# Silu of r at the PSUM banks, key-value products of a head pair in one run, and a token-major end of a hybrid decoder step

## The chip, the cores and the metric

The kernel runs on one core of a Trainium2 chip. The metric is the device time of one execution in microseconds. A profiled execution also has a span, from its first to its last instruction on the core, which is a little shorter than its device time. The engines are called as in the profile: PE does the matrix products (PEld its weight loads), DVE the vector operations, ACT the activation functions, POOL further vector operations without access to PSUM, and SP issues the DMAs.

## What is computed

One inference step of one decoder layer, for 2048 prompt tokens and 8 x 4 sample tokens, width 1024, all in fp32. The mixer projects the normed input into q, k, v, r, a, u and sv. Four heads of gated linear attention run over q, k, v with a decay made from a; four heads of spatial gating run over u and sv.

```
q, k, v, r, a, u, sv = split_cols(xn @ w_in)
logg = log_sigmoid(a @ w_alpha + b_alpha) / GLA_TAU
S_t = diag(exp(logg_t)) S_{t-1} + k_t^T v_t;   o_t = q_t S_t
o = rmsnorm(o, g_gla_out) * silu(r)
z = causal position mixing of rmsnorm(gelu(sv)) within 128 positions;   s_out = gelu(u) * z
h = x + concat(o, s_out) @ w_out
h = h + attention of rmsnorm(h) over 256 memory tokens
c = causal convolution of width 3 of (rmsnorm(h) @ w_gate)
y = rmsnorm(h + (gelu(c) * (rmsnorm(h) @ w_up)) @ w_down, g_final)
```

Besides y, the outputs are the last states of the linear attention, the last two rows of the gate projection, the memory keys and values, and the normed sv of the sample tokens.

## The kernel before, in words

The prompt is worked off in four blocks of 512 tokens (`SB`, `s` = 0 to 3); the 32 sample tokens ride along with block 1 in the mixer and with block 2 in the feed-forward part. Activations lie feature-major, 128 features by 512 tokens to a tile, in eight tiles `B.h[0..7]`. Every large product is made of three products of split fp32 numbers (`mm3`, L92 to L94). A few projections are token-major: `tm_steps` holds four PSUM banks, one for each 128 tokens (c = 0 to 3), and adds up over eight k tiles in four steps (j = 0 to 3) before each bank is evacuated by `evac`. sv, v and r are such projections; r is evacuated by `scaled`, a DVE scaling with the token's rstd.

PSUM has two pools of four banks: `acc` (tag "acc") for the large projections and `mps` (tag "mm") for everything else. SBUF tiles come from pools too: `U` with 49 buffers, `T_` with 6. A new tile of a pool waits until a buffer of that pool is given back.

The linear attention of a block is the list of `gla_steps`. For each pair of heads, p = 0 and 1: `diag`, seven `level`s and `decay` make the local score matrix P (per head), the decayed queries qz (per head), the decayed and transposed keys kt and the chunk decays eb. Then `chunk(p, c)` runs four times, once per 128 tokens: the output products P v and qz S into one "mm" bank (`op`), a DVE copy into B.o, the key-value products kt v of the two heads into another "mm" bank (`kv`), each on 64 of the bank's partitions, and one DVE operation that makes the next state S. The tail (`gtail`) follows: `onorm` squares and sums o, `silu(c)` applies Silu to r in SBUF, `gate(c)` multiplies, `back(h)` transposes the four heads to feature-major `cat[0..3]`. The spatial gating gives `cat[4..7]` through `mix(h)` (`zp`, z, then the split `ch`, `cl`).

The order of the work is written out as a list of steps. `weave` puts the steps of side lists (the gates, the chunks, the mixing, the tail) between the steps of the main list proj + w1, at given places; `run` calls the steps in that order and issues weight loads ahead of them, up to AHEAD = 5 units of cost. The tile framework takes this order as priority and settles at build the order of each engine's instructions by its own estimate of times (`schedule_with_timeline_sim=True`); on the chip each engine and each DMA queue runs its list in that fixed order. The output projection's first half `w1` (`a_wo`, contraction over cat[4..7]) stands right behind the last r step and takes "acc" banks, its second half needs cat[0..3].

The small product for a (`a_fn`, `ap`) gives the decay's input. It is inserted before the last step of sv and takes an "acc" bank. At the start of the program `late_constants` scales the weights for it (wa) on DVE, eight small operations, from a tile loaded by DMA (war).

At the end of block 3 the feed-forward groups go gate, up, down; the last group of two feature tiles is `down_last`: for each half of 256 tokens eight products' groups (feature-major, 256 columns) are added to h, and `final_steps` transposes the half's tokens to PSUM (`yp`), squares them, makes the rstd, scales by it and by g_final and writes y. The last two gate rows (`carry`) are transposed (`ncp`), copied and written by `conv_out_steps`, six steps, ahead of that.

Of the kernel before, what the change touches and what calls it, by code (L numbers as in the profile page):

```python
# [19 lines left out]
D = 1024  # L20
# [17 lines left out]
def hymba_step_kernel(  # L38
# [22 lines left out]
    def U(name, dt=F32):  # L61
        return up.tile([128, TM], dt, tag="U", name=name)
# [7 lines left out]
    def acc(name):  # L70
        return accp.tile([128, 512], F32, tag="acc", name=name)
# [318 lines left out]
    def gcol(nm, k):  # L390
        return cols_of[nm][:, k:k + 1]
# [11 lines left out]
    def late_constants():  # L403
# [15 lines left out]
        for k in range(8):  # L419
            dve.tensor_scalar(wa[:, k, 0:16], war3[:, k], gcol("gmix", k), None, ALU.mult)  # L420

# [384 lines left out]
    def proj_steps(B):  # L806
# [28 lines left out]
        def a_fn():  # L835
            B.aT = T_(f"aT{s}")
            for ci, (c0, cw) in enumerate(chunks_of(sample)):
                ps = acc(f"ap{s}{ci}")
                for k in range(8):
                    pe.matmul(ps[hr[k % 4], :cw], wa[:, k], B.h[k][:, c0:c0 + cw], start=k < 4, stop=k >= 4)  # L840
                act.activation(B.aT[:, c0:c0 + cw], ps[:, :cw], AF.Copy)

        out = tm_steps(w, SV0, xs, sample, ev_tm("sv", lambda o, i, f: act.activation(o, i, AF.Gelu_apprx_tanh, scale=f)), f"ws{s}")
        out.insert(3, Step(a_fn))
        out.append(fm_step(w, K0, xs, sample, ev_fm("k", 0, times), f"wk{s}"))
# [74 lines left out]
    def gla_steps(B):  # L920
# [6 lines left out]
        def gates():  # L927
# [24 lines left out]
            B.lg = lg  # L952
            B.P, B.qz, B.kt, B.eb, B.kms, B.b = {}, {}, {}, {}, {}, {}

# [118 lines left out]

        def chunk(p, c):
            if p == 0 and c == 0:
                B.o = [U(f"o{s}{i}") for i in range(nt)]
            ps = mps(f"op{s}{p}{c}")
            S = state[p]
            cs = slice(c * 128, (c + 1) * 128)
            for hh in range(2):  # L1080
                h = 2 * p + hh
                os_ = slice(hh * 128, (hh + 1) * 128)
                pe.matmul(ps[:, os_], B.P[h][:, cs], B.v[c][:, h * 128:(h + 1) * 128], start=True, stop=False)
                pe.matmul(ps[:, os_], B.qz[h][:, cs], S, start=False, stop=True)
            dve.tensor_copy(B.o[c][:, p * 256:(p + 1) * 256], ps[:, :256])
            kv = mps(f"kv{s}{p}{c}")
            for hh in range(2):
                h = 2 * p + hh
                pe.matmul(kv[hh * 64:(hh + 1) * 64, :128],
                          B.kt[p][:, c * 128 + hh * 64:c * 128 + (hh + 1) * 64],  # L1090
                          B.v[c][:, h * 128:(h + 1) * 128], start=True, stop=True)
            Sn = cp.tile([128, 128], F32, tag=f"S{p}", name=f"S{s}{p}{c}", bufs=2)
            dve.scalar_tensor_tensor(Sn, S, B.eb[p][:, c:c + 1], kv[:, :128], ALU.mult, ALU.add)
            state[p] = Sn
            if s == NSB - 1 and c == 3:
                nc.sync.dma_start(o_state_gla[0, 0, 2 * p:2 * p + 2].rearrange("hh d v -> (hh d) v"), Sn)

# [41 lines left out]

        def silu(c):  # L1140
            n = 128 if c < 4 else NS
            act.activation(B.r[c][:n, :512], B.r[c][:n, :512], AF.Silu)

        def gate(c):
# [311 lines left out]

    def ffn_steps(B, fin=None):
        s, sample = B.s, B.ffn_sample
# [87 lines left out]

        def down_last(f0, half_of):

            def step(half, ws):
                cs = slice(half * 256, (half + 1) * 256)  # L1550
                for m in range(8):
                    wh, wl = ws[m // 4]
                    ms = slice((m % 4) * 128, (m % 4 + 1) * 128)
                    ps = acc(f"d{s}{f0}{m}{half}")
                    for k in range(2):
                        hi, lo = acts[f0 + k]
                        mm3(ps[:, :256], wh[:, k, ms], wl[:, k, ms], hi[:, cs], lo[:, cs], k == 0, k == 1)
                    dve.tensor_tensor(B.h[m][:, cs], ps[:, :256], B.h[m][:, cs], ALU.add)

            def fn(*ws):  # L1560
                for half in range(2):
                    step(half, ws)
                    for st in half_of(half):
                        st.fn()
            return Step(fn, [wready(wdd[f0, 4 * j], f"wd{s}{f0}{j}") for j in range(2)])

# [24 lines left out]
        for f0, nf in GROUPS:  # L1591
            for i in range(0, nf, 2):
                j = (f0 + i) // 2
                here = pend if i == 0 else []
                main += [g_(j), u_(j)] + here if nf == 2 else [g_(j)] + here + [u_(j)]
            if fin and nf == 2:
                pend = [down_last(f0, lambda half: fin[2 * half:2 * half + 2])]
            else:
                pend = [down(f0, nf, m) for m in range(0, 8, 8 // nf)]
# [58 lines left out]
    for s, B in enumerate(blocks):  # L1658
# [18 lines left out]
        steps += weave(sc + x1, (turns[:2], 4, 5), (turns[2:], 8, 8))  # L1677
        fin = final_steps(B)
        fstart, fmain, flast = ffn_steps(B, fin if s == NSB - 1 else None)
        steps += x2 + [xstat, fstart]  # L1680
        sides = []
        if B.mix_sample:
            sides.append((sample_steps(), 1, len(fmain) - 5))
        steps += weave(fmain[:-4], *sides)
        after = fin
        if s + 1 < NSB:
            nxt = blocks[s + 1]
# [39 lines left out]
```

## Time and profile before

| what | us |
|---|---|
| median of 3 runs (range) | 2845.88 (2843.69 to 2846.43) |
| the profiled execution | 2846.04 |
| its span | 2844.3 |
| PE busy | 2814.4 (99%) |
| PEld busy | 2457.6 (86%) |
| DVE busy | 1773.6 (62%) |
| ACT busy | 1047.0 (37%) |
| POOL busy | 542.4 (19%) |

A row of a timeline has the start, the duration, the engine, the line, the operation and its tiles (out<-in), the shape and a count when equal neighbours are merged; in brackets stands the engine's idle time just before it and who ended it. The duration of a product is from its start to its modelled end and overlaps the next one's; the pace of PE is read from the starts. L92 to L94 are the three products of `mm3`. PEclk is the granted clock of PE as a share of the full one.

### The profile page before, as it was taken

Reading aid. Unit: us, or ns where it says so; the run is one execution under the profiler, and the core shown is the slowest. Engines: PE = TensorE matmul, PEld = TensorE weight load, DVE = VectorE, ACT = ScalarE, POOL = GpSimd, SP = SyncE. Lnnn points to the kernel's source line nnn. Section 1 sums busy time; section 2 is a strip of 40 time slices with the busy share of each in tenths; the row PEclk is TensorE's granted clock in tenths of the full one; section 3 lists DMA queues with packets and bytes.
Section 4 is the critical chain, followed back from the end, with each engine's and each line's share of the span. In section 5 each row is a group of like instructions: output and inputs, shape, how many; then the busy total and the mean of one; then the engine's idle time right before and its main releaser. Section 6 shows DMA issues by size and latency. Waiting matters only on the chain.

```text
span 2844.3 us, 45766 instructions
## 1 busy us (share of the span) xinstructions
PE 2814.4 (99%) x17366; PEld 2457.6 (86%) x17366; DVE 1773.6 (62%) x3160; ACT 1047.0 (37%) x1942; POOL 542.4 (19%) x617
## 2 busy tenths in 40 slices
PE   8999999999999999999999999999999999999998
PEld 8788888888888898898888888899999888899998
DVE  6577468777657735555555773666666674565555
ACT  5536334333363424222124443422223543331221
POOL 1002113111110211322220021322221012131221
PEclk9999999999999999999999999999999999999999
DMA  9656679999932245888994215577776323577784
GB/s 304 207 156 199 208 228 332 335 340 329 345 112 77 94 153 178 302 284 291 329 344 161 73 60 181 191 259 257 257 263 213 104 69 119 185 258 269 273 286 173
DMA packets 363920, 625.54 MB, mean 220 GB/s; under 512 B 26730, under 2 KB 235724, under 8 KB 363702
## 3 DMA queue, kind: packets, MB, share of 16 engines
q1 hardware_dynamic: 363702, 622.62, 64.6%
q8 instruction: 138, 2.26, 0.3%
q14 instruction: 80, 0.66, 0.1%
HBM read 497.21 MB, written 125.31 MB: 219 GB/s over the span
## 4 chain that ended last, share of the span: by engine, by line
PE 95%; DVE 2%; DMA 1%; ACT 1%; issue 1%; POOL 0%; SPq 0%; DVEq 0%; POOLq 0%; ACTq 0%
PE d L92 6%; PE d L94 6%; PE d L93 6%; PE a_wo L92 2%; PE a_wo L94 2%; PE a_wo L93 2%; PE sc L94 2%; PE sc L93 2%; PE sc L92 2%; PE a_wx L93 2%; PE a_wx L94 2%; PE a_wx L92 2%; PE s L1022 2%; PE a_wg L92 1%; PE a_wup L92 1%; PE a_wg L93 1%
## 5 line engine op out<-in xcount | busy, mean ns | idle before, releaser
L92 PE MATMUL d<-acth,whi_wd 128*128 128x512 f32 (+2 forms) x720 | 244.6, 340 | 0.5 <-DVE h L1581 0.5
L93 PE MATMUL d<-actl,whi_wd 128*128 128x512 f32 (+2 forms) x720 | 242.5, 337 | 0.0
L94 PE MATMUL d<-acth,wlo_wd 128*128 128x512 f32 (+2 forms) x720 | 242.0, 337 | 0.0
L1581 DVE TENSOR_TENSOR h<-d,h 128x512 f32<-128x512 f32 (+1 forms) x232 | 133.4, 582 | 139.6 <-PE d L94 139.4
L1520 POOL TENSOR_TENSOR c<-c,bc_f 128x512 f32<-128x512 f32 (+1 forms) x88 | 138.5, 1578 | 137.9 <-ACT c L1519 137.2
L94 PEld LDWEIGHTS d<-acth,wlo_wd 128*128 128x128 f32 x720 | 135.4, 188 | 15.3 <-issue 1.2
L92 PEld LDWEIGHTS d<-acth,whi_wd 128*128 128x128 f32 x720 | 135.3, 188 | 14.4 <-DVE h L1581 0.7
L93 PEld LDWEIGHTS d<-actl,whi_wd 128*128 128x128 f32 x720 | 135.6, 188 | 13.8 <-issue 0.4
L1510 ACT ACTIVATE c<-g,colsb 128x512 f32<-128x512 f32 x88 | 71.7, 815 | 203.7 <-DVE g L1479 151.8
L1542 POOL TENSOR_TENSOR c<-r_q_wup,c 128x512 f32<-128x512 f32 (+1 forms) x33 | 59.1, 1790 | 333.5 <-DVE r_q_wup L279 213.1
L92 PE MATMUL a_wo<-ch,h_wo 128*128 128x512 f32 (+1 forms) x320 | 112.7, 356 | 4.5 <-DVE r L828 4.5
L1507 POOL COPY carry<-g 128x2 f32<-128x2 f32 x88 | 30.7, 349 | 436.5 <-DVE g L1479 434.4
L94 PE MATMUL a_wo<-ch,l_wo 128*128 128x512 f32 (+1 forms) x320 | 112.4, 353 | 0.0
L93 PE MATMUL a_wo<-cl,h_wo 128*128 128x512 f32 (+1 forms) x320 | 112.0, 351 | 0.0
L1511 DVE SCALAR_TENSOR_TENSOR c<-g,colsb,c 128x512 f32<-128x512 f32 x88 | 86.0, 977 | 29.3 <-ACT c L1510 28.8
L92 PE MATMUL sc<-whi_qk,woh 128*128 128x512 f32 x256 | 102.1, 399 | 0.0
L92 PE MATMUL a_wx<-pTh,whi_wx 128*128 128x512 f32 x256 | 101.3, 396 | 0.0
L94 PE MATMUL sc<-whi_qk,wol 128*128 128x512 f32 x256 | 101.1, 397 | 0.0
L93 PE MATMUL a_wx<-pTl,whi_wx 128*128 128x512 f32 x256 | 101.1, 395 | 0.0
L93 PE MATMUL sc<-wlo_qk,woh 128*128 128x512 f32 x256 | 101.0, 395 | 0.0
L94 PE MATMUL a_wx<-pTh,wlo_wx 128*128 128x512 f32 x256 | 100.6, 393 | 0.0
L84 ACT ACTIVATE acth<-c 128x512 fp32r<-128x512 f32 (+1 forms) x88 | 55.9, 636 | 110.4 <-DVE c L1542 85.0
(3369 smaller groups left out, 9204.8 us busy)
## 6 DMA issues: line engine op xcount, KB each, us to landing
whi_wd<-wd SPq DMA_DIRECT2D x66, 512.0 KB
wlo_wd<-wd SPq DMA_DIRECT2D x66, 512.0 KB
r_wo<-in_w_out_dram SPq DMA_DIRECT2D x32, 512.0 KB
whi_qk<-qkd SPq DMA_DIRECT2D x32, 512.0 KB
wlo_qk<-qkd SPq DMA_DIRECT2D x32, 512.0 KB
wlo_wx<-vod SPq DMA_DIRECT2D x32, 512.0 KB
whi_wx<-vod SPq DMA_DIRECT2D x32, 512.0 KB
r_wg<-in_w_gate_dram SPq DMA_DIRECT2D x22, 512.0 KB
```

Source lines behind the costliest of these rows:

```text
L84: act.activation(hi, src, AF.Copy)
L92: pe.matmul(ps, wh, xh, start=first, stop=False)
L93: pe.matmul(ps, wh, xl, start=False, stop=False)
L94: pe.matmul(ps, wl, xh, start=False, stop=last)
L1022: pe.matmul(ps3[:, :, c * 64:(c + 1) * 64], kl[:, c * 128:(c + 1) * 128], kr3[:, :, c * 64:(c + 1) * 64], start=True, stop=True)
L1507: pool.tensor_copy(carry[:, f, :], g[:, SB:SB + 2])
L1510: act.activation(c[:, :SB], g[:, 2:SB + 2], AF.Identity, bias=cb, scale=w2)
L1511: dve.scalar_tensor_tensor(c[:, :SB], g[:, 1:SB + 1], w1, c[:, :SB], ALU.mult, ALU.add)
L1520: pool.tensor_tensor(c[:, :T], c[:, :T], B.fbc[:, :T], ALU.mult)
L1542: (dve, pool)[i].tensor_tensor(c[:, :T], q[i], c[:, :T], ALU.mult)
L1581: dve.tensor_tensor(B.h[m + mm][:, cs], ps[:, :cw], B.h[m + mm][:, cs], ALU.add)
```

## The change

Six edits, all in the order or the place of work; the arithmetic is the same but for the end's order of sums.

1. r is evacuated by ACT with Silu, scaled by the token's rstd, straight from the "acc" bank. The DVE scaling and the `silu` steps of the tail are gone.
2. `chunk` becomes `states(p)` and `chunks(p, i)`. `states` does the key-value products of the four chunks of a pair, eight in a row, into one "mm" bank, then the four state updates; the states of the chunks live in a new tile of the U pool. `chunks` does the output products of two chunks into the two halves of one bank, and copies each half.
3. `a_fn` takes an "mm" bank and stands behind all of sv's steps.
4. wa is scaled by POOL instead of DVE.
5. The last down group of block 3 is made token-major: `turn_h` transposes h (before that group's part) to tokens through PSUM and ACT copies, between the steps of the group before; `last_rows` makes the down products with tokens on the partitions, 512 columns each, adds the turned h, sums the squares, and scales and writes a row tile while the next one is computed. For the last row tile, POOL multiplies the first half by g_final before the rstd is known, and ACT scales it.
6. Four of the six steps that write the last gate rows go between the gate and up steps of block 3, the other two behind the last full down group.

```diff
-            dve.tensor_scalar(wa[:, k, 0:16], war3[:, k], gcol("gmix", k), None, ALU.mult)
+            pool.tensor_scalar(wa[:, k, 0:16], war3[:, k], gcol("gmix", k), None, ALU.mult)
...
-                ps = acc(f"ap{s}{ci}")
+                ps = mps(f"ap{s}{ci}")
...
-        out.insert(3, Step(a_fn))
+        out.append(Step(a_fn))
...
-        out += tm_steps(w, R0, xs, sample, ev_tm("r", scaled), f"wr{s}")
+        out += tm_steps(w, R0, xs, sample, ev_tm("r", lambda o, i, f: act.activation(o, i, AF.Silu, scale=f)), f"wr{s}")
...
-        def chunk(p, c):
...
+        def states(p):
+            kv = mps(f"kv{s}{p}")
+            for c in range(4):
+                for hh in range(2):
+                    h = 2 * p + hh
+                    pe.matmul(kv[hh * 64:(hh + 1) * 64, c * 128:(c + 1) * 128],
+                              B.kt[p][:, c * 128 + hh * 64:c * 128 + (hh + 1) * 64],
+                              B.v[c][:, h * 128:(h + 1) * 128], start=True, stop=True)
+            t = U(f"S{s}{p}")
+            B.S[p] = [state[p]] + [t[:, c * 128:(c + 1) * 128] for c in range(3)]
+            state[p] = cp.tile([128, 128], F32, tag=f"S{p}", name=f"S{s}{p}e", bufs=2)
+            for c in range(4):
+                dve.scalar_tensor_tensor(B.S[p][c + 1] if c < 3 else state[p], B.S[p][c], B.eb[p][:, c:c + 1],
+                                         kv[:, c * 128:(c + 1) * 128], ALU.mult, ALU.add)
...
+        def chunks(p, i):
...
+            ps = mps(f"op{s}{p}{i}")
+            for j in range(2):
+                c = 2 * i + j
+                cs = slice(c * 128, (c + 1) * 128)
+                for hh in range(2):
+                    h = 2 * p + hh
+                    os_ = slice(j * 256 + hh * 128, j * 256 + (hh + 1) * 128)
+                    pe.matmul(ps[:, os_], B.P[h][:, cs], B.v[c][:, h * 128:(h + 1) * 128], start=True, stop=False)
+                    pe.matmul(ps[:, os_], B.qz[h][:, cs], B.S[p][c], start=False, stop=True)
+                dve.tensor_copy(B.o[c][:, p * 256:(p + 1) * 256], ps[:, j * 256:(j + 1) * 256])
...
-            out += [lambda p=p, c=c: chunk(p, c) for c in range(4)]
+            out += [lambda p=p: states(p)] + [lambda p=p, i=i: chunks(p, i) for i in range(2)]
...
-        tail = [onorm] + [lambda c=c: silu(c) for c in range(nt)] + [lambda c=c: gate(c) for c in range(nt)]
+        tail = [onorm] + [lambda c=c: gate(c) for c in range(nt)]
...
+        def turn_h(j):
+            for c in range(4):
+                ps = mps(f"hp{c}{j}")
+                for i in range(4):
+                    pe.transpose(ps[:, i * 128:(i + 1) * 128], B.h[4 * j + i][:, c * 128:(c + 1) * 128], ident)
+                t = U(f"ht{c}{j}")
+                act.activation(t[:, :512], ps, AF.Copy)
+                cur["ht", c, j] = t
...
+        def last_rows(*ws):
...
+            def finish(c, ss):
+                for j in range(2):
+                    y = cur["free"] if (c, j) == (2, 1) else T_(f"y{s}{c}{j}")
+                    if c == 3 and j == 0:
+                        act.activation(y[:, :512], early[:, :512], AF.Copy, scale=ss[:, 3:4])
+                    else:
+                        dve.scalar_tensor_tensor(y[:, :512], cur["ht", c, j][:, :512], ss[:, 3:4], gfin[j][:, :512],
+                                                 ALU.mult, ALU.mult)
+                    nc.sync.dma_start(y_prompt[0, s * SB + c * 128:s * SB + (c + 1) * 128, j * 512:(j + 1) * 512], y[:, :512])
...
+            for c in range(4):
...
+                    for k in range(2):
+                        hi, lo = acts[FT - 2 + k]
+                        mm3(ps, hi[:, cs], lo[:, cs], wh[:, k], wl[:, k], k == 0, k == 1)
...
+                    act.activation(junk, y[:, :512], AF.Square, accum_out=ss[:, j:j + 1])
+                    if c == 3 and j == 0:
+                        early = U("yg")
+                        pool.tensor_tensor(early[:, :512], y[:, :512], gfin[0][:, :512], ALU.mult)
...
+            ncs = conv_out_steps(carry, 2, o_state_conv[0, 0], "nc")
+            sides.append((ncs[:4], 30, 36))
...
-            steps += fmain[-4:] + conv_out_steps(carry, 2, o_state_conv[0, 0], "nc") + flast
+            steps += fmain[-4:-2] + flast[:1] + fmain[-2:] + ncs[4:] + flast[1:]
```

More of the change, by code (lines that the diff above doesn't have):

```diff
@@ L952, in gates @@
             B.lg = lg
-            B.P, B.qz, B.kt, B.eb, B.kms, B.b = {}, {}, {}, {}, {}, {}
+            B.P, B.qz, B.kt, B.eb, B.kms, B.b, B.S = {}, {}, {}, {}, {}, {}, {}
         def cums(p):
@@ L1072, in decay @@
                 B.kms[p] = km
-        def chunk(p, c):
[L1075 to L1096, printed above, removed]
@@ new lines, in states @@
+        def states(p):
[12 more added lines that the diff above has]
+                                         kv[:, c * 128:(c + 1) * 128], ALU.mult, ALU.add)
+            if s == NSB - 1:
+                nc.sync.dma_start(o_state_gla[0, 0, 2 * p:2 * p + 2].rearrange("hh d v -> (hh d) v"), state[p])
@@ new lines, in chunks @@
+        def chunks(p, i):
+            if p == 0 and i == 0:
+                B.o = [U(f"o{s}{c}") for c in range(nt)]
+            ps = mps(f"op{s}{p}{i}")
[8 more added lines that the diff above has]
+                dve.tensor_copy(B.o[c][:, p * 256:(p + 1) * 256], ps[:, j * 256:(j + 1) * 256])
@@ L1454, in sample_steps, with ffn_steps @@
                 + project(wo_x[0], of_o, got_o, "so"))
-    def ffn_steps(B, fin=None):
+    def ffn_steps(B, last=False):
         s, sample = B.s, B.ffn_sample
@@ L1545, in upp7 @@
             return seven_step(*w7d["u", j], lambda: B.hn, H, use, f"wup{s}{j}")
[L1547 to L1554, printed above, removed]
-                    for k in range(2):
[L1556 to L1565, printed above, removed]
+        def turn_h(j):
[6 more added lines that the diff above has]
+                cur["ht", c, j] = t
@@ L1595, in ffn_steps @@
                 main += [g_(j), u_(j)] + here if nf == 2 else [g_(j)] + here + [u_(j)]
-            if fin and nf == 2:
-                pend = [down_last(f0, lambda half: fin[2 * half:2 * half + 2])]
+            if last and nf == 2:
+                pend = [Step(lambda j=j: turn_h(j)) for j in range(2)]
+                pend.append(Step(last_rows, [wready(wdd[f0, 4 * j], f"wd{s}{f0}{j}") for j in range(2)]))
             else:
@@ L1683, in hymba_step_kernel @@
             sides.append((sample_steps(), 1, len(fmain) - 5))
+        if s + 1 == NSB:
+            ncs = conv_out_steps(carry, 2, o_state_conv[0, 0], "nc")
+            sides.append((ncs[:4], 30, 36))
         steps += weave(fmain[:-4], *sides)
-        after = fin
         if s + 1 < NSB:
+            after = final_steps(B)
             nxt = blocks[s + 1]
```

31 lines of the change are left out of this document (26 added, 5 removed).

## The prediction

> **What bounds the kernel now.** The page comes first: its span, the engines' busy time and the chain that ended last.
>
> ```profile
> span 2844.3 us, 45766 instructions
> ...
> PE 2814.4 (99%) x17366; PEld 2457.6 (86%) x17366; DVE 1773.6 (62%) x3160; ACT 1047.0 (37%) x1942; POOL 542.4 (19%) x617
> ...
> PE 95%; DVE 2%; DMA 1%; ACT 1%; issue 1%; POOL 0%; SPq 0%; DVEq 0%; POOLq 0%; ACTq 0%
> ```
>
> PE is busy but for 29.9 us. An edit counts only where it ends PE idleness, makes PE's own work shorter, or shortens what follows PE's last product. DVE at 62% and ACT at 37% matter only when one of their instructions is late. Next the waits of PE (line, releaser: us in total, times, longest).
>
> ```profile
> PE a_wo L92 <- DVE r L828: 4.5, 3, 2.0
> ...
> PE ap L840 <- ACT sv L843: 2.3, 1, 2.3
> ...
> PE mkt L567 <- DVE mkf L558: 2.1, 2, 1.8
> ```
>
> These three are what the change touches; the other waits of that view belong to loads at the start and to the end. Last, PE's clock in four stretches of 5 us (after the busy times of five engines stands PEclk, the granted share).
>
> ```profile
> 110.00:115.00 5.00, 4.24 (x19) 1.61 (x20) 0.96 (x3) 4.41 (x12) 0.00 (x0) 0.66 1.00 327
> 970.00:975.00 5.00, 4.67 (x29) 3.36 (x26) 3.27 (x9) 0.66 (x1) 1.63 (x3) 0.66 1.02 339
> 975.00:980.00 5.00, 5.00 (x25) 3.91 (x24) 4.13 (x10) 3.82 (x6) 3.72 (x3) 0.65 0.55 184
> 2343.00:2348.00 5.00, 3.02 (x24) 2.78 (x24) 4.15 (x8) 3.33 (x15) 2.52 (x3) 1.00 0.37 118
> ```
>
> So some of the busy time is slow time: the hole at `ap` (110 to 115) and the end of the gate projection of block 1 (970 to 980) ran at two thirds of the clock, the hole of block 3 (2343 to 2348) did not. Lost by the clock: 0.34 x 5 = 1.7 us, and (0.34 + 0.35) x 5 = 3.45 us.
>
> **The sum's base.** The profiled execution took 2846.04 us, 1.7 more than its span and 0.16 more than the median of the three runs, 2845.88. All terms come off 2846.04.
>
> **Part 1, Silu at the banks.** Block 3, PE first, then DVE, then ACT:
>
> ```profile
> 2339.74 0.39 PE L93 MATMUL t_wr<-l_wr,xh 128*128 128x512 f32 x1
> 2339.97 0.39 PE L94 MATMUL t_wr<-h_wr,xl 128*128 128x512 f32 x1
> ...
> 2343.55 1.95 PE L892 MATMUL zp<-wsT,sv 128*128 128x128 f32 x16
> 2347.48 0.51 PE L92 MATMUL a_wo<-ch,h_wo 128*128 128x512 f32 x1 [1.98 <-DVE r L828]
> ...
> 2346.69 2.71 DVE L828 TENSOR_SCALAR r<-t_wr,xrs 128x512 f32<-128x512 f32 x4
> ...
> 2348.01 0.63 ACT L84 ACTIVATE ch<-z 128x512 fp32r<-128x512 f32 x1 [0.60 <-POOL z L905]
> 2348.66 1.28 ACT L1142 ACT_TABLE_LOAD   x1
> 2349.95 2.20 ACT L1142 ACTIVATE r<-r 128x512 f32<-128x512 f32 x4
> ```
>
> The last gate product starts at 2339.97 and its four "acc" banks stay full until DVE reads them from 2346.69 on; `a_wo` needs one of them and PE stands 1.98 us. The late reading follows the program's order of tiles. The `zp` of heads 2 and 3 run only after the last `op` and `kv`, since all take banks of the four-bank "mm" pool and `chunk` takes two banks eight times; the tiles of r follow those of `ch` in the pool of 49. I read this from the code and the order of the rows; the profile names only the last releaser. After the change a head pair takes three banks instead of eight, so `zp`, z and `ch` come several us earlier, and r is taken by ACT as soon as a row tile's sum is done. Removed: four DVE instructions of 0.68 (2.71/4) and four ACT ones of 0.55 (2.20/4) per block; added: four ACT readings of a bank, which no row shows, between 0.55 and 0.68. The table load of 1.28 stays, now ahead of the bank's release, where the remaining `t_wr` of later row tiles (24 products in the last step, 0.23 apiece by the two rows above, 5.5 us) cover it. If that cover is gone it costs 1.28 and a reading, 2.0 us per block, which is the idleness of today. Queued behind it on ACT are the squares of `onorm`; who waits for those is `gate` and then `back`, and PE has the 96 products of the first half of `a_wo` (22 us) in between. Gain: of 4.5 us idle I take 4.0, of the 3.45 us of slow clock in block 1 a third, 1.2, since much of that stretch is small products that stay. Sum 5.2; bounds 8.0 and, as a loss, the third rival.
>
> The row has the first Silu 1.29 us after the table load's start. The Trainium skill (ScalarE: Activation LUTs, What ACT_TABLE_LOAD costs) gives about 1283 ns for the load and a drain of about 1380 ns besides, 2.66 us per switch, which speaks against putting one ahead of a bank's release. By it four blocks would lose up to 5.5 us more and the sum would be 2837.3, an estimate; the trace agrees on the load and shows no drain behind it.
>
> **Part 2, the decay input `ap`.** Block 0, then block 2 for comparison:
>
> ```profile
> 110.76 2.99 PE L840 MATMUL ap<-h,wa 128*32 128x512 f32 x16 [2.26 <-ACT sv L843]
> 113.68 0.80 PE L92 MATMUL a_wk<-xh,h_wk 128*128 128x512 f32 x1
> ...
> 1548.71 1.92 PE L840 MATMUL ap<-h,wa 128*32 128x512 f32 x16
> 1550.57 0.55 PE L1621 MATMUL yp<-ident,h 128*128 128x128 f32 x3
> ```
>
> `ap` waits for an "acc" bank that ACT's gelu of sv frees, 2.26 us, and then runs 2.92 us instead of 1.86 (1548.71 to 1550.57), in the half-speed stretch of 110 to 115. In an "mm" bank it needs no gelu, so its 1.86 us fill the hole. `a_wk` still waits for the gelu: 0.4 us of the hole stay. I take 1.9 of idleness and the 1.1 us of slow clock: 3.0. Bounds: 0 (the folds of wq hold all "mm" banks until ACT comes to them) and 4.0 (2.26 + 1.7).
>
> **Part 3, key-value products in one run.** Block 3 again, start times; and the counts of `kv`:
>
> ```profile
> 2341.32 0.49 PE L1084 MATMUL op<-S,qz 128*128 128x128 f32 x2
> 2341.64 0.39 PE L1083 MATMUL op<-v,P 128*128 128x128 f32 x2
> 2341.87 0.39 PE L1084 MATMUL op<-S,qz 128*128 128x128 f32 x2
> 2342.09 0.39 PE L1083 MATMUL op<-v,P 128*128 128x128 f32 x2
> 2342.41 0.44 PE L1089 MATMUL kv<-v,kt 128*64 128x128 f32 x4
> 2342.78 0.49 PE L1084 MATMUL op<-S,qz 128*128 128x128 f32 x2
> ...
> L1089 PE MATMUL kv<-v,kt x128: 272/298/323, 205.4 to 2342.6; 128*64 128x128 f32 x128
> ```
>
> Two `op` take 0.22 to 0.23 us among themselves (2341.64, 2341.87), but 0.32 right behind a `kv` (2341.32 to 2341.64) and 0.32 right ahead of one (2342.09 to 2342.41). So entering and leaving the 128*64 form costs 0.10 each, 0.20 per run of `kv`, with up to 0.05 more inside the run, where merged rows can't tell. 128 instructions in fours are 32 runs; after, 8 runs of 16 (4 blocks, 2 pairs). 24 x 0.20 = 4.8 us, which I take; bounds 6.0 (24 x 0.25) and 0 (runs broken again). The chain of four state updates on DVE keeps its instructions; PE waits for it today for under 1 us in all.
>
> What this adds: two chunks now share a bank, so the second chunk's products wait for the copy of the first. The nearest rows are the copy and, at worst, a weight split ahead of it on DVE:
>
> ```profile
> L1085 DVE COPY o<-op x32: 401/419/426, 203.1 to 2343.8; 128x256 f32<-128x256 f32 x32
> ...
> 2341.70 1.22 DVE L85 TENSOR_TENSOR l_wo<-r_wo,h_wo 128x1024 fp32r<-128x1024 f32 x1
> ```
>
> 16 such waits of 0.42 to 1.64 us. The other bank's four products (0.9 us) and the projection's products lie in between; I charge 0.5 us, bounds 0 and 26 (second rival).
>
> **Part 4, the end.** PE, DVE, ACT and SP's queue after the last full down-projection:
>
> ```profile
> 2818.14 1.91 PE L1639 MATMUL ncp<-ident,carry 128*2 128x128 f32 x16
> ...
> 2833.66 1.31 PE L1621 MATMUL yp<-ident,h 128*128 128x128 f32 x8
> ...
> 2818.34 0.69 DVE L1581 TENSOR_TENSOR h<-d,h 128x512 f32<-128x512 f32 x1 [2.08 <-PE d L94]
> ...
> 2839.56 1.41 DVE L1628 SCALAR_TENSOR_TENSOR y<-yp,yss,gf 128x512 f32<-128x512 f32 x2 [0.66 <-POOL yss L299]
> ...
> 2837.20 0.60 ACT L1622 ACTIVATE junk<-yp 128x512 bf16<-128x512 f32 x1
> ...
> 2832.83 8.50 SPq L1629 DMA_DIRECT2D out_dram<-y  x8
> ```
>
> From 2818.14 to 2833.66, 15.5 us, PE does 22 carry transposes, 96 down products of 256 columns and 16 of the 32 output transposes. After, the same work is 22 + 32 transposes at 0.12 (1.91/16), 6.5, and 48 products of 512 columns at 0.23, 11.0: 17.5, so 2.0 later (1.4 if the transposes go at 0.11). Sixteen of the carry transposes go into the gate and up stage, where PE is full as well: moved, not saved. Their four DVE copies and four DMAs go there too; on SP a DMA that waits for its copy holds up the weight loads behind it, which run AHEAD (5) units early, some us of cover. Behind PE: today 2833.66 to 2840.97, 7.3 us, with 16 transposes and two row tiles in it. After, the last product's add 0.69, then square to scaling as in the rows (2837.20 to 2839.56, 2.36), one y of 0.70 and 0.16 of pipeline: 3.9. Saved 3.4, net 1.4; DVE has 3.1 us of work per row tile (two adds, two y, the small ones) against PE's 2.8, so I take 1.2; bounds 2.0 and -0.4. The last two output DMAs are issued one after the other as now. Eight ACT copies of turned h lie beside the 11 us of products; the one POOL product of row tile 3 starts six products before the end and is off the path unless it outlasts the last add and square.
>
> **Part 5, the start.** wa's eight products leave DVE for POOL:
>
> ```profile
> 24.37 1.20 DVE L420 TENSOR_SCALAR wa<-war,colsa 128x16 f32<-128x16 f32 x8 [3.63 <-DMA war<-in_w_in_dram]
> ```
>
> DVE stands 3.63 us for a load with `mkf` queued behind; PE waits for `mkf` 2.1 us in two pieces. POOL has nothing due there, and `ap` needs wa only at 110. I take 0.5, bounds 0 and 2.1.
>
> **Sum:** 5.2 + 3.0 + 4.8 + 1.2 + 0.5 - 0.5 = 14.2, so 2831.8 us.
>
> **The rivals.** First, the banks come free no earlier, because r's tiles still queue behind `ch`: part 1 is lost, 2837.0. For it: r and `ch` stand together in the rows. Against: fewer "mm" banks are asked for.
> Second, slower: the shared bank. If the order fixed at build puts the second chunk's products right behind the first's, and DVE has a split ahead of the copy, PE stands 1.6 us in 16 places, 26 us: 2831.8 + 26 = 2857.8. It decides from 0.9 us per place (14.2/16). For it: in-order DVE, and splits next to the copies in the rows. Against: projection products are at hand in most places.
> The Trainium skill (PSUM — Partial Sum Buffer, Terms) says that two engines may not use one bank's quadrant at once; no run here shows what would happen, only that the program must wait.
> Third, Silu late: ACT keeps today's order, squares, `ch`, table load, Silu. Then the first bank is free at 2350.5 (2349.95 + 0.55) instead of 2347.4 (2346.69 + 0.68), 3.1 later in four blocks: 2837.0 + 12.5 = 2849.5.
> Fourth, the change does not do what it says: `kv` is broken into as many runs as now, 2836.6.
>
> **How the numbers follow.** Forecast 0.56 (own range 2826 to 2836), first rival 0.12, fourth 0.07, third 0.15, second 0.10. About 0.2%, 5.7 us, is what a measurement can tell, so faster means below 2840.2: 0.56 + 0.12 + 0.07 = 0.75; same 0.15 from the third; slower 0.10 from the second. The low end is all upper bounds, 8.0 + 4.0 + 6.0 + 2.0 + 2.1 = 22.1: 2824. The high end, 2847, takes the third rival in where it holds in three of four blocks (2837.0 + 3 x 3.1 = 2846.3); left out are the second and a part of the third, under 0.2.
>
> **What would show it.** Part 1: no wait of `a_wo` for r or Silu over 0.5 us, clock 1.00 around 975. Part 2: no wait of `ap`, full clock at 110 to 115. Part 3: eight merged rows of `kv` x16. Part 4: last product about 1.4 to 2.0 later against the down-projection's end, last y about 4 us behind it. Wrong would be a new PE wait for `o<-op`, for Silu, or for a state update of several us in all.

## The result: slower, by 0.6%

The changed kernel takes 2861.41 us (median of 4 runs, 2859.81 to 2864.19), the one before 2844.78 us. The ratio is 1.006, with a 95% interval of 1.0047 to 1.0073: 13 to 21 us slower. The forecast was 2831.8 us, 14 us faster. The profiled execution of the changed kernel took 2859.81 us against 2846.04 before, 13.8 us more, and so did its span. The profile's page, its span, the busy times and the chain that ended last:

```profile
span 2858.1 us, 45636 instructions
...
PE 2813.9 (98%) x17318; PEld 2459.5 (86%) x17318; DVE 1758.5 (62%) x3126; ACT 1046.9 (37%) x1947; POOL 555.2 (19%) x626
...
PE 93%; ACT 2%; DVE 2%; DMA 2%; issue 1%; POOL 1%; SPq 0%; POOLq 0%; DVEq 0%; ACTq 0%
```

PE is as busy as before (2814.4), in a span that is longer by 13.8 us. The idleness has grown. Where it sits, by the waits of PE:

```profile
PE a_wo L92 <- ACT r L850: 15.9, 4, 4.4
...
PE mkt L567 <- DVE mkf L558: 2.2, 2, 1.5
...
PE t_wv L92 <- DVE q L847: 2.0, 1, 2.0
...
PE s L1022 <- DVE o L1105: 0.8, 1, 0.8
```

The wait of `a_wo` that was to go, 4.5 us for DVE's r, is now 15.9 us for ACT's r, four times out of four. The wait of `ap` is gone, and one of `t_wv` for q stands in its place. Block 3 shows the first (timeline of PE, DVE, POOL and ACT):

```profile
2350.24 1.06 PE L892 MATMUL zp<-wsT,sv 128*128 128x128 f32 x8
...
2351.60 0.39 PE L94 MATMUL t_wr<-h_wr,xl 128*128 128x512 f32 x1
...
2352.49 0.39 PE L1104 MATMUL op<-S,qz 128*128 128x128 f32 x2
2356.76 0.50 PE L92 MATMUL a_wo<-ch,h_wo 128*128 128x512 f32 x1 [3.88 <-ACT r L850]
...
2351.33 0.75 DVE L895 SCALAR_TENSOR_TENSOR z<-zp,colsb,bsb 128x512 f32<-128x512 f32 x1 [0.47 <-PE zp L892]
...
2352.16 1.27 POOL L905 TENSOR_TENSOR z<-z,u 128x512 f32<-128x512 f32 x1 [1.48 <-DVE z L895]
...
2353.81 0.61 ACT L84 ACTIVATE ch<-z 128x512 fp32r<-128x512 f32 x1
2354.32 0.29 ACT L855 ACTIVATE junk<-o 128x128 bf16<-128x128 f32 x1
...
2354.73 1.28 ACT L850 ACT_TABLE_LOAD   x1
2356.02 2.42 ACT L850 ACTIVATE r<-t_wr,xrs 128x512 f32<-128x512 f32 x4
```

Silu stands on ACT behind the last `ch`; `ch` waits for POOL's product, that for DVE's z, that for the last `zp`. Then come one square, the table load and Silu, and only then is a bank free. The last product of the gate projection had started at 2351.60, so the first Silu (2356.02) comes more than 4 us after its input was done. Before, r was read by DVE behind its own z and one small step of the rstd of o (`rt`, 0.56 us), whose squares ACT had already done; DVE didn't wait for POOL or ACT there.

The clock adds to this. Behind the hole PE runs at two thirds of its clock for 5 us (after the busy times stands PEclk):

```profile
2357.00:2362.00 5.00, 5.00 (x16) 3.95 (x16) 0.59 (x1) 2.94 (x11) 0.00 (x0) 0.66 0.01 5
2362.00:2367.00 5.00, 5.00 (x23) 4.05 (x22) 2.81 (x8) 1.06 (x1) 2.90 (x1) 1.00 0.01 2
```

The whole difference, read from the first product of each stage in the two traces:

| stretch | before, us | after, us | difference |
|---|---|---|---|
| start to the first `a_wu` (block 0) | 181.65 | 179.91 | -1.7 |
| first `a_wu` to first `sc`, the sum of four blocks | 520.5 | 532.0 | +11.5 |
| first `t_ws` to first `a_wu`, block 1 | 93.4 | 96.0 | +2.6 |
| the same, block 3 | 85.2 | 84.1 | -1.1 |
| first `d` of block 3 to the span's end | 305.0 | 307.5 | +2.5 |
| all other stretches | | | 0.0 |

In the second row PE's idleness grew from 5.8 to 18.5 us (+12.7, of which `a_wo` 11.4), the time lost at half clock from 3.4 to 8.5 us (+5.1), and `kv` and `op` got 4.8 us shorter. These add up to 13.0; why the row shows 1.5 us less isn't explained. In the fifth row, of the +2.5 us about 1.8 lie in gate, up and down products that the change doesn't touch: 60 products of a feed-forward group (`a_wg..S`, `a_wup..S`) take 7.13 us there against 7.05 before. With Part 4 alone they take 7.05 again; the cause stays open.

### The profile page after: what moved, and what is told of

The parts are those of the page before. It is cut to its first block, busy times and chain, and to the rows that moved or that the text cites. A ratio compares the mean times of both kernels' runs of the same rounds, so it can differ in the third digit from the quotient of the medians.

```text
span 2858.1 us, 45636 instructions
## 1 busy us (share of the span) xinstructions
PE 2813.9 (98%) x17318; PEld 2459.5 (86%) x17318; DVE 1758.5 (62%) x3126; ACT 1046.9 (37%) x1947; POOL 555.2 (19%) x626
## 4 chain that ended last, share of the span: by engine, by line
PE 93%; ACT 2%; DVE 2%; DMA 2%; issue 1%; POOL 1%; SPq 0%; POOLq 0%; DVEq 0%; ACTq 0%
PE d L92 5%; PE d L94 5%; PE d L93 5%; PE a_wo L92 2%; PE a_wo L93 2%; PE a_wo L94 2%; PE sc L94 2%; PE sc L93 2%; PE sc L92 2%; PE a_wx L92 2%; PE a_wx L93 2%; PE a_wx L94 2%; PE s L1022 2%; PE a_wg L92 1%; PE a_wup L92 1%; PE a_wup L93 1%
## 5 line engine op out<-in xcount | busy, mean ns | idle before, releaser
L92 PE MATMUL d<-acth,whi_wd 128*128 128x272 f32 (+1 forms) x688 | 235.3, 342 | 0.2 <-DVE h L1623 0.2
L93 PE MATMUL d<-actl,whi_wd 128*128 128x272 f32 (+1 forms) x688 | 234.1, 340 | 0.0
L94 PE MATMUL d<-acth,wlo_wd 128*128 128x272 f32 (+1 forms) x688 | 233.3, 340 | 0.0
L1623 DVE TENSOR_TENSOR h<-d,h 128x512 f32<-128x512 f32 (+1 forms) x232 | 133.5, 582 | 144.5 <-PE d L94 144.5
L94 PEld LDWEIGHTS d<-acth,wlo_wd 128*128 128x128 f32 x688 | 129.3, 188 | 15.4 <-issue 1.2
L92 PEld LDWEIGHTS d<-acth,whi_wd 128*128 128x128 f32 x688 | 129.4, 188 | 14.2 <-DVE h L1623 0.5
L93 PEld LDWEIGHTS d<-actl,whi_wd 128*128 128x128 f32 x688 | 129.5, 188 | 13.7 <-issue 0.4
L92 PE MATMUL a_wo<-ch,h_wo 128*128 128x512 f32 (+1 forms) x320 | 116.3, 364 | 15.9 <-ACT r L850 15.9
L1516 DVE SCALAR_TENSOR_TENSOR c<-g,colsb,c 128x512 f32<-128x512 f32 x88 | 85.9, 976 | 29.5 <-ACT c L1515 28.9
```

The lines of the kernel that those rows point to most:

```text
L92: pe.matmul(ps, wh, xh, start=first, stop=False)
L93: pe.matmul(ps, wh, xl, start=False, stop=False)
L94: pe.matmul(ps, wl, xh, start=False, stop=last)
L1516: dve.scalar_tensor_tensor(c[:, :SB], g[:, 1:SB + 1], w1, c[:, :SB], ALU.mult, ALU.add)
L1623: dve.tensor_tensor(B.h[m + mm][:, cs], ps[:, :cw], B.h[m + mm][:, cs], ALU.add)
```

## The experiments

Each kernel was compared with the kernel before on the same chip. In labels, a_ is the changed kernel with an edit, b_ the kernel before with one, c_ a combination of the change's parts with the early tiles that come below. One us is 0.035% of the time.

**Is it Part 1?** Theory T says that Silu is late: r's tiles are handed out behind those of the last `ch`, and on ACT this place costs POOL's product, the split, the table load and Silu itself. Rival R says that the merged products push the gate projection back. One run undoes Part 1 alone, one makes it alone.

```diff
 a_r_dve (the changed kernel):
-ev_tm("r", lambda o, i, f: act.activation(o, i, AF.Silu, scale=f))
+ev_tm("r", scaled)            # and silu(c) in the tail again
 b_silu (the kernel before): the reverse
```

> The changed kernel with Part 1 alone undone: r is scaled by DVE out of the banks, Silu runs in SBUF as before. Theory T (Silu is late: r's tiles come behind the last ch, then a table load and a Silu pass before a bank is free): a_wo's wait falls from 15.9 us to 4 to 8 us in all, the half-speed stretches behind it go, time 2842 to 2848. Rival R (the merged key-value products push the gate projection's end back, and that is what a_wo waits for): the wait stays above 12 us and the time above 2856.

> The kernel before with Part 1 alone. Theory T: a_wo's wait grows from 4.5 to 12 to 17 us in all and half-speed stretches follow it, time 2854 to 2864. Rival R (the loss comes from the merged products): wait 2 to 6 us, time 2841 to 2848.

The waits of PE for r, first with Part 1 undone, then with it alone:

```profile
PE a_wo L92 <- DVE r L828: 5.3, 4, 2.4
```

```profile
PE a_wo L92 <- ACT r L850: 14.5, 4, 5.2
```

Measured: 2842.88 us, ratio 0.9993 (0.9984 to 1.0002), with Part 1 undone; 2860.02 us, ratio 1.0049 (1.0036 to 1.0062), with Part 1 alone. Part 1 costs 10 to 18 us by itself, which is nearly the whole loss. R falls. One point of theory T's expectation was missed: with Part 1 undone the half-speed stretches didn't all go. From the first `a_wu` to the first `sc` of the four blocks 6.8 us were lost to them (8.5 in the changed kernel, 3.4 before), in an execution that was the slowest of its eleven.

**Is it the tiles' order, or ACT's queue?** In the order of instructions that the build settles, the tiles of the pools acc, mm and T_ are written for the first time in the order in which the code first uses them, and so are those of the pool U behind the set-up. r comes after the third and fourth `ch` in the code. One run puts the first use of r's tiles ahead of them:

```diff
 a_r_first (the changed kernel):
         def mix(h):
+            if h == 2:
+                B.r = [U(f"r{s}{c}") for c in range(nt)]
+                for t in B.r:
+                    pool.memset(t[:, 543:544], 0.0)
```

(543 is a column that r doesn't use; the later request of r's tiles is left out.)

> The changed kernel with one thing added: the four tiles of r are asked for and touched (one column each, on POOL) ahead of the tiles of the third and fourth ch. Nothing is taken off ACT. Theory T: Silu of row tiles 0 to 2 runs ahead of the last ch, a_wo's wait falls from 15.9 to below 5 us in all, time 2840 to 2848. Rival Q (ACT's own queue makes Silu late: squares, splits and a table load of 1.28 us, whatever the tiles): the wait stays at 12 to 16 us, time 2857 to 2864.

The top of PE's waits:

```profile
PE colpsa L384 <- POOL mf L354: 2.7, 1, 2.7
PE mtp L525 <- DMA mx<-in_mem_prompt_dram: 2.3, 2, 1.8
PE t_wv L92 <- DVE q L847: 2.1, 1, 2.1
```

Measured: 2838.07 us, 2 us below the range of theory T, ratio 0.9974 (0.9964 to 0.9984). The wait of `a_wo` for r is gone, with the same Silu, table load and squares on ACT. T holds, Q falls, and this version is 0.26% faster than the kernel before.

**How much of the wait is the table load?** A run with a plain scaled copy in place of Silu: Silu of r is left out of the computation, so its output is another one and only its time is read.

```diff
 a_copy (the changed kernel):
-act.activation(o, i, AF.Silu, scale=f)
+act.activation(o, i, AF.Copy, scale=f)
```

> The changed kernel with a plain copy, scaled by the token's rstd, in place of Silu: Silu of r is left out of the computation, and with it the table loads. Theory T (each bank release carries one table load of 1.28 us and no more): a_wo's wait falls from 15.9 to 10 to 11.5 us in all, time 2850 to 2857. If a switch costs 2.66 us as the Trainium skill has it (ScalarE: Activation LUTs, What ACT_TABLE_LOAD costs), the wait falls to 5 to 6 us. If the place behind ch is all that matters, it stays above 14 us.

The wait, and block 3 on ACT and PE:

```profile
PE a_wo L92 <- ACT r L850: 10.3, 4, 3.0
```

```profile
2347.51 0.61 ACT L84 ACTIVATE ch<-z 128x512 fp32r<-128x512 f32 x1
...
2348.32 2.39 ACT L850 ACTIVATE r<-t_wr,xrs 128x512 f32<-128x512 f32 x4
...
2349.04 0.52 PE L92 MATMUL a_wo<-ch,h_wo 128*128 128x512 f32 x1 [2.46 <-ACT r L850]
```

Measured: 2851.82 us, ratio 1.0023 (1.0014 to 1.0032). The wait falls by 5.6 us, 1.4 for each of four table loads. The row of the load says 1.28, so a load costs the bank's release next to no more than itself. The Trainium skill (ScalarE: Activation LUTs, What ACT_TABLE_LOAD costs) has 2.66 us per switch; the wait doesn't agree. The other 10.3 us stay without any load on the path; 4.5 of them were there before, and by the run above, where all of it went, they belong to the place behind `ch`.

**The other parts, each alone on the kernel before.**

> The kernel before with Part 3 alone. By the prediction 4.3 us faster than before: 2839 to 2843. Rival R: it makes the gate projection end later and a_wo wait, 2846 or more. Rival B (two chunks in one bank): PE waits for the copy of o by several us in all, 2846 or more.

b_kv, Part 3 alone: 2843.88 us, ratio 0.9998 (0.9989 to 1.0006), that is -3.1 to +1.7 us where -4.3 was forecast. The waits of PE:

```profile
PE a_wo L92 <- DVE r L828: 5.2, 3, 2.6
...
PE s L1022 <- DVE o L1105: 0.8, 1, 0.8
```

In the changed kernel, whose `kv` are the same, the run in block 3 is whole, at 64 ns per instruction (a plain fp32 product is two instructions here, so x16 are eight products):

```profile
2343.22 1.09 PE L1080 MATMUL kv<-v,kt 128*64 128x128 f32 x16
```

From start to start, without PE's waits, `kv` and `op` took 43.47 us before and 38.63 us in b_kv and in the changed kernel, 4.8 less. Against that, from the first `a_wu` to the first `sc` of the four blocks, PE stands 2.1 us longer in b_kv: 0.7 more at `a_wo`, 0.8 for a copy of o (the shared bank) and 0.8 ahead of `vop`, less some small waits. One more half-speed stretch of 3.41 us took another 1.7 us in this execution. So the wait for r takes back only a small part of what the products give. In block 3 `a_wo` starts 69.1 us after the stage's first `a_wu` and 70.9 before: the chain ahead of it ends earlier, if not by as much as PE does.

> The kernel before with Part 2 alone (ap in the other pool, behind all of sv's steps). By the prediction 3.0 us faster. Reading P of the changed kernel's trace: the hole of 2.26 us at ap goes, but t_wv waits about 2.0 us for q in block 1, so at most 1 us faster; if that wait isn't there, it came from another part.

b_ap, Part 2 alone: 2846.09 us, ratio 1.0004 (0.9995 to 1.0013), -1.4 to +3.7 us where -3.0 was forecast. The hole at `ap` goes (`a_wk` starts 2.7 us earlier against the stage's start), and the new one is there:

```profile
PE t_wv L92 <- DVE q L847: 2.0, 1, 2.0
```

It is in block 1, where DVE does twenty scalings of sv ahead of the reading of q. DVE in the changed kernel:

```profile
853.46 6.07 DVE L880 TENSOR_SCALAR sv<-sv,srs 128x128 f32<-128x128 f32 x20 [1.80 <-POOL srs L299]
859.45 0.42 DVE L847 SCALAR_TENSOR_TENSOR q<-a_wq,bc_x 128x272 f32<-128x272 f32 x1
```

Reading P holds.

> The kernel before with Part 4 alone (token-major end, carry rows among the gate and up steps). By the prediction 1.2 us faster than before. Reading E of the changed kernel's trace (the y of earlier row tiles stand ahead of the last add on DVE, which has more to do per row tile than PE): 2 to 3 us slower, with 9 to 10.5 us behind the last product.

b_end, Part 4 alone: 2847.1 us, ratio 1.0005 (0.9996 to 1.0014), -1.1 to +4.0 us. By time this tells neither the forecast's gain of 1.2 us nor reading E's 2 to 3 us of loss from nothing. In its trace the stretch from the first `d` of block 3 to the span's end is 0.7 us longer than before (305.7 and 305.0), and 10.0 us stand behind the last product, as reading E expects. The changed kernel's end shows why, on PE, DVE and POOL:

```profile
2848.04 0.40 PE L94 MATMUL dr<-whi_wd,actl 128*128 128x512 f32 x1
...
2843.57 1.42 DVE L1577 SCALAR_TENSOR_TENSOR y<-ht,yss,gf 128x512 f32<-128x512 f32 x2
...
2847.68 2.41 DVE L1577 SCALAR_TENSOR_TENSOR y<-ht,yss,gf 128x512 f32<-128x512 f32 x2
...
2850.09 0.68 DVE L1595 TENSOR_TENSOR htl<-dr,ht 128x512 f32<-128x512 f32 x1
...
2851.48 0.75 DVE L1577 SCALAR_TENSOR_TENSOR y<-ht,yss,gf 128x512 f32<-128x512 f32 x1 [0.65 <-POOL yss L299]
2852.14 0.75 DVE L1577 SCALAR_TENSOR_TENSOR ht<-ht,yss,gf 128x512 f32<-128x512 f32 x1
2852.81 0.15 DVE L1602 TENSOR_TENSOR yss<-yss 128x1 f32<-128x1 f32 x1
...
2853.80 0.75 DVE L1577 SCALAR_TENSOR_TENSOR y<-htl,yss,gf 128x512 f32<-128x512 f32 x1 [0.66 <-POOL yss L299]
...
2847.84 1.70 POOL L1601 TENSOR_TENSOR yg<-ht,gf 128x512 f32<-128x512 f32 x1 [0.78 <-DVE ht L1597]
```

The last product ends at 2848.4; its add comes at 2850.09, behind two y of row tile 1; the sum of squares at 2852.81, behind two y of row tile 2. From the last product's start to the last y's end are 6.5 us, and 10.1 to the span's end. The two y of row tile 1 took 2.41 us beside POOL's product, and the two of row tile 0 took 1.42 without one.

**An end without adds.** To test that DVE's work sets the end, h is turned by products with the identity into the bank of the down products; squares and y read the bank, as before the change. The run also scales each row tile at once instead of behind the next one's adds, and makes the early product with g_final on DVE instead of POOL.

```diff
 c_end_psum (the changed kernel with the early tiles of r):
+mm3(ps, ..., wh[:, 0], wl[:, 0], True, False)
+for i in range(4):
+    pe.matmul(ps[:, i * 128:(i + 1) * 128], B.h[4 * j + i][:, cs], ident, start=False, stop=False)
+mm3(ps, ..., wh[:, 1], wl[:, 1], False, True)
-dve.tensor_tensor(y[:, :512], ps, y[:, :512], ALU.add)     # and turn_h with its eight ACT copies
 c_old_end (the same kernel with the early tiles): Part 4 undone
```

> The changed kernel with the tiles of r asked for early and another end: h is turned by four products with the identity into the same bank as the down products, so that DVE has no add and ACT no copy, and the squares and y read the bank. Reading E (DVE's work per row tile sets the end): 6 to 7.5 us behind the last product instead of 10, so 2.5 to 4 us faster than with the change's end. If PE or the output DMAs set the end, within 1 us of it.

> The changed kernel with the tiles of r asked for ahead of the third ch, and with Part 4 undone (the end of before). Reading E: 2 to 3 us faster than the same with the new end (which was 2838.1 beside a before of 2843.7), so a ratio to before of 0.9965 to 0.997. By the prediction's Part 4 it would be 1.2 us slower than with the new end, 0.998.

Last product, its identity products, and the last y of c_end_psum, whose span is 2834.6 us:

```profile
2826.77 1.05 PE L1575 MATMUL dr<-ident,h 128*128 128x128 f32 x8
...
2828.12 0.40 PE L94 MATMUL dr<-whi_wd,actl 128*128 128x512 f32 x1
...
2830.34 0.75 DVE L1589 SCALAR_TENSOR_TENSOR y<-dr,yss,gf 128x512 f32<-128x512 f32 x1 [0.66 <-POOL yss L299]
```

Measured: c_end_psum 2836.82 us, ratio 0.9971 (0.9959 to 0.9983); c_old_end 2835.59 us, ratio 0.9966 (0.9954 to 0.9979); with the change's end the ratio was 0.9974. Behind the last product stand 6.5 us instead of 10.1, as reading E expects, but the time is no better than with the old end; by time the three ends can't be told apart. PE gave it back: a product with the identity that adds up runs as two instructions (x8 above are four products), 64 in 6.5 us, where the 32 transposes of the change's end took 2.9. Both differences are 3.6 us. The expectation of 2.5 to 4 us failed on that. Since the run moves more than the adds, it shows that DVE and POOL's work behind the last product can be shortened by 3.6 us, not how much of that the adds alone cost.

**What are the early tiles worth without the rest?**

```diff
 b_r_first: the kernel before + the early tiles of r, r still scaled by DVE
 b_silu_first: the same + Part 1
 b_kv_r_first: the kernel before + Part 3 + the early tiles of r
 c_r_first_dve: Parts 2, 3, 5 + the early tiles, r scaled by DVE, old end
 c_no_ap: Parts 1, 3, 5 + the early tiles, old end
```

> The kernel before, with nothing changed but the place at which the tiles of r are asked for (ahead of the third ch); r is still scaled by DVE and Silu still runs in SBUF. Theory O (the order of the tiles is worth the gain, the engine that takes r is not): a_wo's wait falls from 4.5 to under 2 us in all, ratio to before 0.997 to 0.999. Theory S (Silu at the banks carries a gain of its own once it stands early): the wait stays near 4 us here, ratio 0.999 to 1.001.

> The kernel before with Part 1 and the early tiles of r. Theory O: the same as with the early tiles alone, within 0.1%, a ratio of 0.997 to 0.999, against 1.0049 for Part 1 without the early tiles. Theory S: 0.2% or more below the run with the early tiles alone.

Measured: 2857.32 us, ratio 1.0045 (1.0032 to 1.0057), and 2855.07 us, ratio 1.0039 (1.0026 to 1.0052). Both theories missed the level: the early tiles alone make the kernel before slower. Only that the two runs stand within 0.1% of each other is as theory O has it. The wait of `a_wo` for r is gone there, too, but another stands at the top, and block 3 of b_r_first shows where it comes from (PE and POOL):

```profile
PE otp L1159 <- DVE o L1152: 7.8, 6, 2.0
```

```profile
2345.48 0.50 PE L92 MATMUL a_wo<-ch,h_wo 128*128 128x512 f32 x1
...
2355.60 1.09 PE L92 MATMUL a_wo<-ch,h_wo 128*128 128x512 f32 x4
2358.63 0.30 PE L1159 MATMUL otp<-ident,o 128*128 128x128 f32 x1 [1.95 <-DVE o L1152]
...
2352.96 1.29 POOL L909 TENSOR_TENSOR z<-z,u 128x512 f32<-128x512 f32 x1 [10.93 <-DVE rt L298]
2354.21 2.90 POOL L299 TENSOR_TENSOR ors<-rt,neghalf 128x16 f32<-128x16 f32 x1
2357.08 1.26 POOL L909 TENSOR_TENSOR z<-z,u 128x512 f32<-128x512 f32 x1
```

`a_wo` begins while `op` and `kv` are still running and uses up what can be done before the last `ch` are there. The `zp` of heads 2 and 3 still stand behind all of `op` and `kv`: they start 70.1 and 71.1 us after the stage's first `a_wu`, later than the 67.0 and 67.9 of before. On POOL the rstd of o, 2.90 us, has got ahead of the last z. What PE then waits for are three transposes of the gated o (`otp`), which wait for the gates on DVE, and these for that rstd. From the first `a_wu` to the first `sc` of the four blocks PE stands idle for 11.5 us against 5.8 before, and 8.5 against 3.4 us are lost at half clock. Part 3 takes three banks per head pair instead of eight, which lets `zp` run between: in b_kv_r_first they start at 59.3 and 65.0 us, and the wait of `otp` is gone. That it is the number of banks is read from the code; no run changed that number alone.

> The kernel before with Part 3 and the early tiles of r, nothing else (r scaled by DVE, Silu in SBUF, the end of before). Alone they gave ratios of 0.9998 and 1.0045. Theory I (Part 3 frees the banks that the products zp wait for, so that ch is ready when the early tiles let the output projection begin): together 0.996 to 0.998, no wait of a_wo over 1 us. If the two simply add up: 1.003 to 1.006.

> Parts 2, 3 and 5 with the early tiles of r, the end of before, and r scaled by DVE with Silu in SBUF. Theory O: within 0.1% of the same with Silu at the banks, whose ratio was 0.9966. Theory S: 0.2% or more above it.

> Parts 1, 3 and 5 with the early tiles of r and the end of before, without Part 2. If Part 2 is worth nothing (its 2.6 us at ap paid back by the wait of t_wv for q in block 1 and elsewhere), within 0.1% of the same with Part 2, whose ratio was 0.9966; the wait of ap (about 2 us) is back and that of t_wv is gone. If Part 2 is worth the 3.0 us of the prediction, a ratio of 0.9975 to 0.998.

Measured: b_kv_r_first 2833.82 us, ratio 0.9962 (0.9949 to 0.9976); c_r_first_dve 2833.56 us, ratio 0.9965 (0.9952 to 0.9977); c_no_ap 2835.29 us, ratio 0.9969 (0.9959 to 0.998). Waits of PE in b_kv_r_first:

```profile
PE ap L840 <- ACT sv L843: 1.9, 1, 1.9
...
PE a_wo L93 <- POOL cl L85: 1.2, 1, 1.2
```

Theory I holds in its time: -0.02% and +0.45% alone, -0.38% together, about 11 us. (One wait of `a_wo`, for `cl` in block 1, is 1.2 us where none over 1 was expected.) Whether ACT with Silu or DVE takes r then makes no difference (0.9966 and 0.9965), nor does Part 2 (0.9966 and 0.9969). Two edits are enough for a version as fast as any here: Part 3, and r's tiles ahead of the third `ch`. (The version without Part 5, b_kv_r_first, is no slower than those with it.)

## Why the prediction was wrong

**Part 1** (-5.2 forecast, +10 to +18 measured alone) is the step that failed, at "r is taken by ACT as soon as a row tile's sum is done". What stood before it was right: `zp`, z and `ch` do come earlier. The last eight `zp` start at 2350.24 in the changed trace and near 2344.4 before; this stage began 9.5 us later (first `a_wu` of block 3 at 2286.1 and 2276.6), so they come 3.7 us earlier within it. But r's place in the list of tiles didn't move, and the engine did. On DVE the place behind `ch` cost only z, which DVE itself makes; on ACT it costs what ACT waits for there. The table load, taken as covered by the last gate products, came 3 us after them (2354.73 against 2351.60). "If that cover is gone it costs 1.28 and a reading, 2.0 us per block" has about the size of what blocks 2 and 3 show, 3.9 us instead of 1.98, but blocks 0 and 1 went from 0.5 and 0 to 4.4 and 3.7. With the load taken out altogether 10.3 us of the wait stayed, 5.8 more than before, and with r's tiles ahead of the third `ch` none did, the load still there. So of the growth of 11.4 us the load makes 5.6 and the place behind `ch` the rest.

**The third rival** described this order word for word (squares, `ch`, table load, Silu) and priced it at 3.1 us per block, 12.5 in all; the wait grew by 11.4 in the changed kernel. With Part 1 alone the wait of blocks 2 and 3 grew by 3.2 each. It had 0.15. What spoke for it was in the prediction: r and `ch` stand together in the rows, and the table load is on the way. The first rival (2837.0, 0.12) also had r's tiles still behind `ch`, but at no loss: it saw the place, not what ACT waits for there. It was to give 2849.5 because the other parts were to bring 9.0 us beside it, and because it had no term for the clock: 5.1 us.

**The clock**: Part 1 took 1.2 us of gain from it. Beside each of the four longer holes stands a half-speed stretch; that is a loss where a gain stood. The stretch at `ap`, of which Part 2 took 1.1 us, is gone; but b_end, which keeps that wait, has none there either, so this isn't shown to be the edit's work.

**Part 2** (-3.0; alone -1.4 to +3.7): the hole went nearly as worked out, 2.6 to 2.7 us. What was late next was named only for block 0. The same edit in block 1 frees PE to reach `t_wv` before DVE has read q, 2.0 us.

**Part 3** (-4.8, and +0.5 for the shared bank): eight runs of 16, and 4.8 us less from start to start, exactly the term. PE waits for the copy of o 0.8 us in all, so the second rival fell. Yet alone the part gives -3.1 to +1.7. The term was right; what the sum lacked are the waits that come late instead (0.7 us more at `a_wo`, 0.8 ahead of `vop`) and the clock (1.7 us in the profiled execution). Together with the early tiles of r the same part lets PE gain.

**Part 4** (-1.2; alone -1.1 to +4.0 by time, +0.7 by its trace): the term that failed is the chain behind the last product, 3.9 us in the forecast and 6.5 in the trace, counted from that product's start (6.1 from its end). PE's own part ended about 1.5 us later in b_end, where 1.4 to 2.0 was worked out. The prediction saw that DVE has 3.1 us per row tile against PE's 2.8 and took off 0.2 us for it. Two row tiles' y stood in its way, 1.65 us ahead of the add and 1.2 ahead of the sum, and POOL's product, judged "off the path unless it outlasts the last add and square", slowed two of them by 1.0 us.

**Part 5** (-0.5): PE waits for `mkf` 2.2 us, as before (2.1). It wasn't tried alone. **The fourth rival** (`kv` broken) fell.

## What to carry to other kernels

In a program built like this one, an operation that moves to another engine keeps its place in the order of tiles, and what matters is what the new engine waits for just ahead of that place. Before a bank's release is given to ACT, read which instruction of ACT stands before it and what releases that one; and when a stage is made shorter ahead of a chain that ends last, the gain comes only with the edit that lets the chain end earlier: here two edits worth -0.02% and +0.45% were worth -0.38% together.

## What the runs showed of the hardware

**Half-speed stretches often stand beside holes shorter than 3.4 us, but not always.** In the sixteen profiles of this case (before, after and fourteen runs; the set-up's first 60 us and the end left out) the granted clock is either full or one half, in stretches of 3.41 us or a multiple, 1.7 us lost for each. Of PE's holes of 3.6 us and more, 6 of 6 had such a stretch begin within 4 us of their end; of those between 2.2 and 3.0, 10 of 12; of those between 1.9 and 2.2, 8 of 24. The Trainium skill (TensorE: Matmul & The Clock Gate, HAM oscillation — how this bites in real kernels) warns of gaps over about 3.4 us; here most gaps of 2.2 us had such a stretch beside them. The reverse doesn't hold: 23 of the 47 stretches begin with no hole of 1.9 us or more within 4 us, 16 of these between 910 and 980 us, in block 1. So a hole isn't the only thing that a stretch can come with. This is an observation over all kernels; no run set the length of a hole alone.

**DVE and POOL.** The pair of y that ran beside POOL's product of two SBUF tiles took 2.41 instead of 1.42 us, and before the change, where y was read from a bank, there was no such pair. In the changed trace, `c<-g,colsb,c` (L1516, two inputs in SBUF) takes 0.74 us at median alone and 1.22 where POOL is at work for most of it, while the add `h<-d,h` (L1623, one input in a bank) takes 0.69 and 0.68. The Trainium skill (SBUF — State Buffer, Who interferes with whom) says that a DVE instruction with two SBUF inputs contends with a GpSimd one that reads SBUF; the trace agrees. Moving an operand of DVE from a bank to SBUF, as Part 4 does, makes it open to this.

**A merged run of 128*64 products costs less apiece.** Sixteen `kv` instructions of 128*64 (eight products) take 1.02 us from the first start to the next product's, entering and leaving included, 64 ns apiece, against 0.37 us for four (92 ns).
